# Sparse attention's second half in a given order on TensorE, with fixed score banks, and an earlier end of the state-space preparation

## The chip, the cores and the metric

The kernel runs on one NeuronCore of a Trainium2 chip. A core has TensorE for matrix products and transposes (PE; its weight loads stand in the profile as PEld), VectorE (DVE), ScalarE (ACT), GpSimd (POOL), the queue engine SyncE (SP), which issues most of the DMAs, and 16 DMA engines. Each engine works through its own queue in order, and semaphores tie the queues together. The metric is the device time of one launch in microseconds (us), lower is better.

## The reference, cut to what matters

The program is one block with a dilated-window attention and a pooling branch, followed by two layers of a second block. For 512 tokens of width 1024, all in float32, the stages that matter here are these two of the second block.

```python
# layer 0: sparse attention, 16 heads of 64, rows in 4 blocks of 128 queries
s = einsum('bqhd,bqkhd->bqhk', q, k[idx]) * HEAD_DIM_2 ** -0.5   # idx: the chosen keys
s = where(valid, s, NEG); p = softmax(s)
o = einsum('bqhk,bqkhd->bqhd', p, v[idx]); x = x + g_m * (o @ attn_w_out)
x = x + g_f * conv_ffn(h, ...)           # up, 3-tap convolution, silu gate, down
# layer 1: state-space mixer, then conv_ffn again
decay = exp(a_re * dt); ab = decay * (cos + i sin)(a_im * dt); bb = coef * b
x_t = ab * x_{t-1} + bb @ u_t;  y_t = Re(c @ x_t) + d * u_t
x = x + g_m * glu(gelu(y));  x = x + g_f * conv_ffn(h, ...)
```

In the kernel the choice of keys is a bias per query block (0 for a chosen key, -1e30 for another) that is added to the scores of all keys up to the block's end.

## The kernel before, in words

Activations lie feature-major: X is 8 tiles of 128 features x 512 tokens. A large product takes both operands in two parts (high and low) and adds three products per pair, at lines 260 to 262 in `mm3`; `gemm` does 24 of these for one 128x1024 weight tile and 18 for a 128x768 one. `weight` (lines 239 to 247) loads a tile on the SP queue, ACT makes the high part `wh`, DVE the low part `wl`. There are 4 raw buffers and 3 pairs of weight buffers, so the loads run some tiles ahead.

**The order of work.** The source is traced in order, and a scheduler then places the instructions of each engine by its own model of times; `tc.issue_after` ties an instruction on one engine behind another one. On the chip each engine follows the order that came out. Work in the background is a generator: `pump` (line 223), called once per `weight`, advances it by `rate` steps, and `finish` runs off what is left.

**Sparse attention** (`dsa`). For a head pair `pr` (0 to 7) and a query block `n` (3 to 0, with W = 128(n+1) keys) a unit is: `scores` (line 899), two products of 64 rows into two PSUM banks (L905), on DVE bias and row maximum (L914), a small operation for the exponent's shift (L919), on ACT exp with its row sum (L920), on DVE a reciprocal (L921), on POOL the scaling (L922); then `values` (line 932), transposes (L939), a copy to SBUF by ACT for one head and DVE for the other (L942, L944), the value products (L950), and ACT and DVE make the high and low part of the result (L955, L956). `attend` (line 960) runs `scores` of a unit and `values` of the unit two before. Pairs 0 to 3 run between the projections of the second half of q, k and v (PSUM pool pb); pairs 4 to 7 follow (scores in pool pa), then the 8 output products with `awo` (line 990).

**Preparation for layer 1** (`ssm_prep`, line 1060) computes the discrete system, then for each of the 8 feature tiles k fills `res` and `taps` and writes them to a DRAM tile: 8 transposes (L1195), 8 products in 4 column strips (L1201), a 1.5 MB write (L1212) and 16 small ones (L1216). By the source it yields some 100 steps. It is background of layer 0's feed-forward `conv_ffn(0)`, whose two loops take 44 up and 24 down weight tiles:

```python
bg.append(ssm_prep(sp, dp, rho))
rate[0] = 1.0
nxt = SumSq()
conv_ffn(0, up, acc, nxt)
finish()
```

**State-space mixer** (`s5`, line 1219). The matrices come back as `Rf` and `Rb_` (R in the trace; k = 0 to 2 by the ACT queue, the others by SP, L1229, L1231). The norm of X is: squares on ACT (L282), column sums on PE (L314), small steps on DVE (L297 to L336), a broadcast on PE (L319), a copy `Rb` (L327). Then `ahead` scales and shifts a tile (L1257 or L1259, L1261), PE reorders it (L1245), ACT copies it to U (L1278), and PE multiplies U by the matrices (L1284), the first product of the mixer proper.

## Time and profile before

| | |
|---|---|
| three runs | 2416.22, 2419.20, 2420.52 us; median 2419.2 |
| profiled execution | 2419.24 us, its span 2417.3 us (1.9 us lie around it) |
| PE busy | 2316.2 us (96%), weight loads 1882.7 us (78%) |
| DVE, ACT, POOL busy | 1436.1 us (59%), 876.1 us (36%), 503.0 us (21%) |
| mean granted clock of TensorE | 0.978 |
| chain that ended last | PE 87%, DVE 6%, DMA 3% |

An engine's busy time is the union of its instructions' spans. A PE instruction's end is modelled, so that a PE that waits a little between short products can still show as busy; start times are the better guide there, and the idle time of the weight loads. A line such as L260 belongs to a helper and stands for many stages, so stages are told apart by stretches of time: the second half of the attention is 1362 to 1432 us, layer 0's feed-forward 1468 to 1846, the mixer's start 1846 to 1889, the mixer 1889 to 2041.

### The profile page before, as it was taken

The numbers are of one execution on the slowest core, as the hardware profiler recorded it, in microseconds if no ns is written. First come the engines' busy times: TensorE is split into PE (matmuls) and PEld (weight loads), VectorE is DVE, ScalarE is ACT, GpSimd is POOL, SyncE is SP. The second block draws the span as 40 slices with busy tenths as digits, with TensorE's granted clock in tenths as the row PEclk, the third lists the DMA queues.
The fourth block names the chain that finished last, engine by engine and source line by source line (L and its number), as shares of the span: only waits on it lengthen the run. The fifth ranks groups of instructions, "written<-read, shape, count | busy, mean of one in ns | idle before, by whom it ended". The sixth has DMA issues, their size and how long they took to land.

```text
span 2417.3 us, 30042 instructions
## 1 busy us (share of the span) xinstructions
PE 2316.2 (96%) x11288; PEld 1882.7 (78%) x11288; DVE 1436.1 (59%) x2575; ACT 876.1 (36%) x1374; POOL 503.0 (21%) x462
## 2 busy tenths in 40 slices
PE   7999999999999999998999998999997699999999
PEld 6888888977888888887676577888786687888887
DVE  6655555456675555446797649747476664544443
ACT  3322233533333223234334644425254432433332
POOL 2312022241112212033001221302022520111111
PEclk9999999999999999998999999999998899999999
DMA  5444445323444444322221112333335622232332
GB/s 190 157 157 148 148 136 171 115 90 107 152 153 139 149 156 148 122 88 72 79 62 44 36 46 86 96 126 127 121 112 184 243 66 88 87 96 96 96 96 79
DMA packets 95618, 281.88 MB, mean 117 GB/s; under 512 B 11377, under 2 KB 16369, under 8 KB 93425
## 3 DMA queue, kind: packets, MB, share of 16 engines
q1 hardware_dynamic: 92160, 272.48, 34.9%
q10 hardware_dynamic: 3312, 7.48, 0.9%
q8 instruction: 89, 1.46, 0.2%
q14 instruction: 57, 0.46, 0.1%
HBM read 263.14 MB, written 16.78 MB: 116 GB/s over the span
## 4 chain that ended last, share of the span: by engine, by line
PE 87%; DVE 6%; DMA 3%; issue 1%; ACT 1%; POOL 1%; SPq 1%; ACTq 0%; DVEq 0%; POOLq 0%
PE pa L260 27%; PE pa L261 27%; PE pa L262 27%; DMA raw<-in_ada 1%; PE pb L950 1%; PE pb L939 1%; PE pa L905 1%; DMA dr<-sm 1%; DVE wl L246 1%; PE pb L905 1%; SPq L1216 1%; ACT wh L245 0%; PE pb L314 0%; PE pa L557 0%; PE pb L1284 0%
## 5 line engine op out<-in xcount | busy, mean ns | idle before, releaser
L245 ACT ACTIVATE wh<-raw 128x1024 fp32r<-128x1024 f32 (+2 forms) x380 | 392.1, 1035 | 856.4 <-PE pa L261 680.5
L260 PE MATMUL pa<-x,wh 128*128 128x512 f32 x1736 | 679.5, 393 | 14.4 <-ACT x L343 8.1
L261 PE MATMUL pa<-x,wh 128*128 128x512 f32 x1736 | 680.4, 392 | 4.5 <-DVE x L344 4.5
L262 PE MATMUL pa<-x,wl 128*128 128x512 f32 x1736 | 677.7, 391 | 0.5 <-DVE wl L246 0.5
L246 DVE TENSOR_TENSOR wl<-raw,wh 128x1024 fp32r<-128x1024 f32 (+2 forms) x380 | 494.1, 1302 | 244.8 <-ACT wh L245 236.1
L260 PEld LDWEIGHTS pa<-x,wh 128*128 128x128 f32 x1736 | 327.7, 189 | 85.9 <-ACT x L343 8.1
L261 PEld LDWEIGHTS pa<-x,wh 128*128 128x128 f32 x1736 | 327.6, 189 | 75.6 <-DVE x L344 7.7
L262 PEld LDWEIGHTS pa<-x,wl 128*128 128x128 f32 x1736 | 327.7, 189 | 68.8 <-DVE wl L246 1.0
L261 PE MATMUL pa<-u,wh 128*128 128x512 f32 x704 | 274.7, 391 | 0.0
L260 PE MATMUL pa<-u,wh 128*128 128x512 f32 x704 | 273.7, 392 | 0.0
L262 PE MATMUL pa<-u,wl 128*128 128x512 f32 x704 | 273.1, 391 | 0.0
L368 DVE SCALAR_TENSOR_TENSOR ada<-raw,c,ada 128x512 f32<-128x512 f32 x168 | 130.7, 778 | 220.2 <-DMA raw<-in_ada 219.3
L1013 POOL TENSOR_TENSOR t<-t,t 128x512 f32<-128x512 f32 x44 | 70.8, 1610 | 534.7 <-ACT t L1012 534.7
L402 POOL TENSOR_TENSOR t<-t,t 128x512 f32<-128x512 f32 x44 | 70.5, 1601 | 497.7 <-DVE t L401 272.3
L260 PE MATMUL pa<-wh,x 128*128 128x512 f32 (+1 forms) x384 | 151.0, 401 | 14.6 <-DVE t L805 6.1
L260 PEld LDWEIGHTS pa<-u,wh 128*128 128x128 f32 x704 | 132.2, 188 | 29.8 <-ACT wh L245 1.3
L262 PEld LDWEIGHTS pa<-u,wl 128*128 128x128 f32 x704 | 132.2, 188 | 28.9 <-issue 0.4
L261 PEld LDWEIGHTS pa<-u,wh 128*128 128x128 f32 x704 | 132.3, 188 | 28.3 <-POOL u L406 0.2
L262 PE MATMUL pa<-wh,x 128*128 128x512 f32 (+1 forms) x384 | 150.5, 394 | 0.0
L261 PE MATMUL pa<-wl,x 128*128 128x512 f32 (+1 forms) x384 | 149.7, 390 | 0.0
L1023 DVE SCALAR_TENSOR_TENSOR x<-pa,c,x 128x512 f32<-128x512 f32 x48 | 35.4, 748 | 137.7 <-PE pa L262 137.7
L288 POOL TENSOR_TENSOR acc<-acc,t 128x512 f32<-128x512 f32 x45 | 75.4, 1681 | 179.8 <-ACT t L282 169.4
(365 smaller groups left out, 2739.9 us busy)
## 6 DMA issues: line engine op xcount, KB each, us to landing
raw<-in_ada SPq DMA_DIRECT2D x96, 512.0 KB, 3.8
raw<-in_u SPq DMA_DIRECT2D x88, 512.0 KB, 3.5
raw<-in_f1u SPq DMA_DIRECT2D x44, 512.0 KB, 3.8
raw<-in_f2u SPq DMA_DIRECT2D x44, 512.0 KB, 3.6
raw<-in_d SPq DMA_DIRECT2D x32, 512.0 KB, 3.5
raw<-in_aq SPq DMA_DIRECT2D x28, 512.0 KB, 3.8
dr<-res SPq DMA_DIRECT2D x8, 1536.0 KB, 7.1
raw<-in_wpg SPq DMA_DIRECT2D x20, 512.0 KB, 3.6
```

What stands on the lines that cost most here:

```text
L245: S.activation(h[:, :w], r[:, :w], AF.Copy)
L246: eng.tensor_tensor(l[:, :w], r[:, :w], h[:, :w].bitcast(F32), op=ALU.subtract)
L260: E.matmul(ps, ah, bh, start=first, stop=False)
L261: E.matmul(ps, ah, bl, start=False, stop=False)
L262: E.matmul(ps, al, bh, start=False, stop=last)
L288: G.tensor_tensor(self.sums[0], self.sums[0], sq, op=ALU.add)
L368: V.scalar_tensor_tensor(acc, r[:, j * T : (j + 1) * T], kk, acc, op0=ALU.mult, op1=ALU.add)
L402: G.tensor_tensor(b, a, b, op=ALU.mult)
L905: E.matmul(ps[e][:, :W], QT[pr][base : base + 64, n * P : (n + 1) * P], KTT[pr][base : base + 64, :W], start=True, stop=True,)
L939: E.transpose(p[:, j * P : (j + 1) * P], s[:, j * P : (j + 1) * P], ident)
L1013: G.tensor_tensor(b, a, b, op=ALU.mult)
L1023: V.scalar_tensor_tensor(X[m], p, MOD[i][:, 40 + m : 41 + m], X[m], op0=ALU.mult, op1=ALU.add)
```

## The change

In the second half of the attention (pairs 4 to 7) three things change. Score banks are two fixed pairs, taken once from pool pa and used in turn (`pairs`). `values` is split into `turn` (transposes and copies) and `mix` (value products), and PE gets a written order by `tc.issue_after`: scores of unit u, transposes of unit u-3, value products of unit u-4. The exponents of these pairs go to tiles of pool `du` instead of the ring `s` of 5. In both halves the two heads of a unit share the small tile `mx`: one DVE operation of 128x2 for both shifts and one for both reciprocals, after both maxima and both exponents; the maximum of head 1 is taken before that of head 0. Apart from that the background rate of `ssm_prep` goes from 1.0 to 1.7 steps per weight tile.

```diff
@@ scores
-                    ps = [psb() if pr < 4 else psa() for _ in range(2)]
+                    if pr < 4:
+                        ps = [psb() for _ in range(2)]
+                    else:
+                        ps = pairs[(4 * pr + n) % 2]
...
+                    ss = [ds_.tile([P, T], F32, name=nm("s"), tag="s", bufs=5) if pr < 4 else ut() for _ in range(2)]
+                    mx = ds_.tile([P, 4, 2], F32, name=nm("mx"), tag="mx", bufs=4)
+                    for e in (1, 0):
+                        V.tensor_tensor_reduce(
+                            out=ss[e][:, :W], in0=ps[e][:, :W], in1=bias[n], scale=1.0, scalar=-3e38,
+                            op0=ALU.add, op1=ALU.max, accum_out=mx[:, 0, e : e + 1],
+                        )
+                    sc = rq[:, n, 2 * pr : 2 * pr + 2]
+                    V.scalar_tensor_tensor(mx[:, 1], mx[:, 0], -1.0, sc, op0=ALU.mult, op1=ALU.mult)
                     for e in range(2):
...
+                        S.activation(
+                            ss[e][:, :W], ss[e][:, :W], AF.Exp, bias=mx[:, 1, e : e + 1], scale=sc[:, e : e + 1],
+                            accum_out=mx[:, 2, e : e + 1],
                         )
...
+                    V.reciprocal(mx[:, 3], mx[:, 2])
+                    for e in range(2):
+                        G.tensor_scalar(ss[e][:, :W], ss[e][:, :W], mx[:, 3, e : e + 1], 1.0, op0=ALU.mult, op1=ALU.mult)
+                    return ss, last
@@ after the projections
-                for pr in range(4, 8):
-                    for n in (3, 2, 1, 0):
-                        attend(pr, n)
-                while pend:
-                    values(*pend.pop(0))
+                pairs += [[psa() for _ in range(2)] for _ in range(2)]
+                tail = [(pr, n) for pr in range(4, 8) for n in (3, 2, 1, 0)]
+                last, turned = None, []
...
+                while tail or pend or turned:
+                    if tail:
+                        with after():
+                            ss, last = scores(*tail[0])
+                        pend.append((*tail.pop(0), ss))
+                    if len(pend) > 3 or not tail:
...
+                        with after():
+                            pts, last = turn(*pend[0])
+                        turned.append((*pend.pop(0)[:2], pts))
+                    if len(turned) > 1:
+                        with after():
+                            last = mix(*turned.pop(0))
@@ the program's end
                 bg.append(ssm_prep(sp, dp, rho))
-                rate[0] = 1.0
+                rate[0] = 1.7
```

In the order of PE inside the attention's second half, before: score products are L905 (pa), transposes L939, value products L950.

```order
L905 MATMUL pa_10857<-du_9654,du_10169 128x256
L950 MATMUL pb_10819<-pt_10812,du_10479 64x128
L939 MATMUL pb_10844<-c_102,s_10756 128x128
L905 MATMUL pa_10858<-du_9654,du_10169 128x256
L950 MATMUL pb_10819<-pt_10817,du_10479 64x128
L950 MATMUL pb_10819<-pt_10812,du_10480 64x128
L950 MATMUL pb_10819<-pt_10817,du_10480 64x128
L939 MATMUL pb_10848<-c_102,s_10763 128x128
L905 MATMUL pa_10900<-du_9654,du_10169 128x128
L950 MATMUL pb_10852<-pt_10846,du_10479 64x128
L939 MATMUL pb_10875<-c_102,s_10795 128x128 x4
L905 MATMUL pa_10901<-du_9654,du_10169 128x128
```

Between the two score products of a unit (pa_10857 and pa_10858, pa_10900 and pa_10901) stand value products and transposes of other units.

And with the change (L909, L944 and L960 are the same three):

```order
L944 MATMUL pb_10756<-c_102,du_10645 128x128
L944 MATMUL pb_10758<-c_102,du_10646 128x128
L960 MATMUL pb_10764<-pt_10730,du_10431 64x128
L960 MATMUL pb_10764<-pt_10732,du_10431 64x128
L960 MATMUL pb_10764<-pt_10730,du_10432 64x128
L960 MATMUL pb_10764<-pt_10732,du_10432 64x128
L909 MATMUL pa_10447<-du_9642,du_10133 128x128
L909 MATMUL pa_10448<-du_9642,du_10133 128x128
L944 MATMUL pb_10784<-c_102,du_10677 128x128 x4
L944 MATMUL pb_10789<-c_102,du_10678 128x128 x4
L960 MATMUL pb_10798<-pt_10760,du_10431 64x128
L960 MATMUL pb_10798<-pt_10762,du_10431 64x128
```

The two score products of a unit (pa_10447 and pa_10448) now stand side by side, and so do its transposes and its value products.

PE at the end of layer 0's feed-forward, before. L262 is the last product of the feed-forward, L1195 and L1201 are the preparation of tiles 5 to 7, L314 and L319 the norm.

```order
L262 MATMUL pa_14521<-u_14256,wl_14518 128x512
L1195 MATMUL pb_14624<-c_102,pB_14605 128x128 x4
L1195 MATMUL pb_14630<-c_102,pB_14606 128x128 x4
L1201 MATMUL pb_14636<-mC_14607,pB_14605 32x128 x4
L1201 MATMUL pb_14636<-mC_14608,pB_14606 32x128 x4
L1195 MATMUL pb_14740<-c_102,pB_14721 128x128 x4
L1195 MATMUL pb_14746<-c_102,pB_14722 128x128 x4
L1201 MATMUL pb_14752<-mC_14723,pB_14721 32x128 x4
L1201 MATMUL pb_14752<-mC_14724,pB_14722 32x128 x4
L1195 MATMUL pb_14802<-c_102,pB_14783 128x128 x4
L1195 MATMUL pb_14808<-c_102,pB_14784 128x128 x4
L1201 MATMUL pb_14814<-mC_14785,pB_14783 32x128 x4
```

Of the eight rounds of preparation, the last three stand behind the feed-forward's last product; the third begins with the last three of these rows.

And with the change (the preparation's lines would be L1227 and L1233):

```order
L260 MATMUL pa_14699<-u_14488,wh_14695 128x512
L261 MATMUL pa_14699<-u_14489,wh_14695 128x512
L262 MATMUL pa_14699<-u_14488,wl_14696 128x512
L314 MATMUL pb_14770<-c_78,acc_14518 128x1 x4
L314 MATMUL pb_14770<-c_78,t_14691 128x1 x4
L314 MATMUL pb_14770<-c_78,t_14719 128x1 x4
L319 MATMUL pb_14799<-c_102,c_14787 128x128 x4
L1277 MATMUL pb_14828<-t_14822,c_102 32x128 x16
```

The three rounds are gone from there; the last round now stands 11 weight tiles before the feed-forward's end, and all eight lie inside.

ACT at the same place, before: L327 is the copy of the norm's broadcast, L1261 the scaled tiles, the DMAs are the loads of R for k = 0 to 2, L1278 the copy to U.

```order
L327 ACTIVATE rb_14928<-pb_14923 128x512
L1261 ACTIVATE t_14946<-t_14944,c_108,c_8103 128x512
L1261 ACTIVATE t_14950<-t_14948,c_108,c_8103 128x512
L1261 ACTIVATE t_14983<-t_14981,c_108,c_8103 128x512
L1261 ACTIVATE t_15037<-t_15035,c_108,c_8103 128x512
L1229 DMA R_14850<-dr_12986 128x2048
L1231 DMA R_14852<-dr_12986 128x1536
L1229 DMA R_14854<-dr_13276 128x2048
L1231 DMA R_14856<-dr_13276 128x1536
L1229 DMA R_14858<-dr_13876 128x2048
L1231 DMA R_14860<-dr_13876 128x1536
L1278 ACTIVATE U_14954<-pb_14952 128x512
```

The six loads stand behind the scaled tiles and in front of the first U.

And with the change (L245 is the high part of the third tile of `glu`, L282 the square of the last X tile, L1317 a copy of the decay rates):

```order
L245 ACTIVATE wh_15597<-raw_15595 128x1024
L1261 DMA R_14726<-dr_12398 128x2048
L1263 DMA R_14728<-dr_12398 128x1536
L282 ACTIVATE t_14719<-x_100 128x512
L1261 DMA R_14730<-dr_12556 128x2048
L1263 DMA R_14732<-dr_12556 128x1536
L1261 DMA R_14734<-dr_13000 128x2048
L1263 DMA R_14736<-dr_13000 128x1536
L1317 ACTIVATE rt_14762<-c_11281 128x4x127
L1317 ACTIVATE rt_14763<-c_11281 128x4x127
L327 ACTIVATE rb_14804<-pb_14799 128x512
L1293 ACTIVATE t_14822<-t_14820,c_108,c_8103 128x512
```

Now they stand behind a weight copy, in front of the norm's last square or right behind it.

## Rows read from the trace of the kernel before

**Rows 1.** stretches: us, PE, PEld, DVE, ACT, POOL busy (count), PEclk, DMA share, GB/s.
```profile
1362.00:1407.00 45.00, 43.34 (x281) 25.31 (x280) 28.64 (x147) 30.98 (x93) 15.41 (x29) 0.96 0.00 1
...
1470.00:1846.00 376.00, 375.06 (x1708) 304.18 (x1707) 254.11 (x519) 158.53 (x228) 82.37 (x49) 1.00 0.35 114
1846.00:1889.00 43.00, 16.06 (x132) 12.06 (x130) 20.12 (x67) 16.92 (x30) 3.94 (x9) 0.56 0.59 213
```

**Rows 2.** timeline at the seam: start us, us, engine, line, operation [idle before <-releaser].
```profile
1845.17 0.39 PE L262 MATMUL pa<-u,wl 128*128 128x512 f32 x1
...
1845.42 1.06 ACT L245 ACTIVATE wh<-raw 128x1024 fp32r<-128x1024 f32 x1 [0.41 <-PE pa L261]
...
1847.35 0.74 DVE L1023 SCALAR_TENSOR_TENSOR x<-pa,c,x 128x512 f32<-128x512 f32 x1
```

**Rows 3.** the same timeline, further on.
```profile
1871.19 2.05 PE L319 MATMUL pb<-c,c 128*128 128x128 f32 x8 [3.90 <-DVE c L306]
...
1873.97 0.69 DVE L1257 TENSOR_TENSOR t<-x,pb 128x512 f32<-128x512 f32 x1 [2.63 <-ACT rb L327]
1874.76 4.91 ACT L1261 ACTIVATE t<-t,c,c 128x512 f32<-128x512 f32 x4 [0.89 <-DVE t L1257]
...
1876.12 1.93 PE L1245 MATMUL pb<-t,c 128*32 128x128 f32 x32 [2.88 <-ACT t L1261]
...
1879.06 0.33 ACTq L1229 DMA_DIRECT2D R<-dr  x1
...
1888.64 0.60 ACT L1278 ACTIVATE U<-pb 128x512 f32<-128x512 f32 x1 [8.97 <-issue]
...
1889.29 3.78 PE L1284 MATMUL pb<-U,R 128*128 128x128 f32 x16 [11.24 <-ACT U L1278]
```

**Rows 4.** timeline of the norm before the feed-forward of layer 1.
```profile
2043.74 0.63 ACT L282 ACTIVATE t<-x 128x512 f32<-128x512 f32 x1 [1.15 <-DVE x L1371]
...
2044.42 1.05 PE L314 MATMUL pb<-c,t 128*128 128x1 f32 x8 [1.06 <-ACT t L282]
...
2047.89 2.07 PE L319 MATMUL pb<-c,c 128*128 128x128 f32 x8 [2.42 <-DVE c L306]
```

**Rows 5.** PE timeline around one round of preparation inside the feed-forward.
```profile
1786.31 0.39 PE L262 MATMUL pa<-x,wl 128*128 128x512 f32 x1
1786.55 1.03 PE L1195 MATMUL pb<-c,pB 128*128 128x128 f32 x8
...
1787.65 0.39 PE L261 MATMUL pa<-x,wh 128*128 128x512 f32 x1
...
1792.66 0.39 PE L262 MATMUL pa<-x,wl 128*128 128x512 f32 x1
1792.98 0.64 PE L1201 MATMUL pb<-mC,pB 128*32 128x128 f32 x16
...
1793.89 0.40 PE L261 MATMUL pa<-x,wh 128*128 128x512 f32 x1
```

**Rows 6.** PE timeline, a score pair of the first half.
```profile
1241.84 1.13 PE L905 MATMUL pb<-du,du 64*128 64x512 f32 x4
```

**Rows 7.** PE timeline, score products of the second half.
```profile
1390.70 0.70 PE L905 MATMUL pa<-du,du 64*128 64x256 f32 x2
...
1394.31 1.12 PE L905 MATMUL pa<-du,du 64*128 64x512 f32 x2
```

**Rows 8.** lines of 1362 to 1407 us: busy us, mean ns, idle before <-releasers.
```profile
L920 ACT ACTIVATE s<-s,mx,sm 128x512 f32<-128x512 f32 x8 | 6.5, 813 | 4.5 <-DVE mx L919 2.3 <-PE pb L939 1.7 <-DVE mx L921 0.5
...
L922 POOL TENSOR_SCALAR s<-s,mx 128x512 f32<-128x512 f32 x8 | 5.6, 697 | 9.7 <-DVE mx L921 5.1 <-DVE mx L919 4.6
L914 DVE CUSTOM_DVE_ANT_0 s<-pa,sm 128x512 f32<-128x512 f32 x8 | 5.5, 688 | 2.1 <-PE pa L905 1.3 <-PE pb L939 0.8
```

**Rows 9.** a line of DVE inside the feed-forward, 1470 to 1846 us.
```profile
L1037 DVE TENSOR_TENSOR st<-sm,ca 128x128 f32<-128x128 f32 x12 | 4.2, 354 | 0.0
```

**Rows 10.** the same line behind the feed-forward, 1846 to 1889 us.
```profile
L1037 DVE TENSOR_TENSOR st<-sm,ca 128x128 f32<-128x128 f32 x4 | 1.1, 277 | 0.0
```

More of the change, by code (lines that the diff above doesn't have):

```diff
@@ L897, in project @@
                             S.activation(dst[4 * o + i][:, b * P : (b + 1) * P], p[:, i * P : (i + 1) * P], AF.Copy)
+                pairs = []
                 def scores(pr, n):
                     W = (n + 1) * P
-                    units = []
-                    ps = [psb() if pr < 4 else psa() for _ in range(2)]
+                    if pr < 4:
+                        ps = [psb() for _ in range(2)]
+                    else:
+                        ps = pairs[(4 * pr + n) % 2]
                     for e in range(2):
                         base = 64 * e
-                        E.matmul(
+                        last = E.matmul(
                             ps[e][:, :W], QT[pr][base : base + 64, n * P : (n + 1) * P], KTT[pr][base : base + 64, :W],
@@ L930, in carry, with turn, mix @@
                     S.activation(X[k], X[k], AF.Copy, scale=col("fn", k))
-                def values(pr, n, units):
+                def turn(pr, n, units):
                     W = (n + 1) * P
-                    pts = []
+                    ps, pts = [], []
                     for e in range(2):
-                        s = units[e]
                         p = psb()
                         for j in range(n + 1):
-                            E.transpose(p[:, j * P : (j + 1) * P], s[:, j * P : (j + 1) * P], ident)
+                            last = E.transpose(p[:, j * P : (j + 1) * P], units[e][:, j * P : (j + 1) * P], ident)
+                        ps.append(p)
+                    for e in range(2):
                         pt = ds_.tile([P, T], F32, name=nm("pt"), tag="pt", bufs=4)
                         if e == 0:
-                            S.activation(pt[:, :W], p[:, :W], AF.Copy)
+                            S.activation(pt[:, :W], ps[e][:, :W], AF.Copy)
                         else:
-                            V.tensor_copy(pt[:, :W], p[:, :W])
+                            V.tensor_copy(pt[:, :W], ps[e][:, :W])
                         pts.append(pt)
+                    return pts, last
+                def mix(pr, n, pts):
                     po = psb()
@@ L949, in values @@
                             hd = 2 * pr + e
-                            E.matmul(
+                            last = E.matmul(
                                 po[64 * e : 64 * e + 64, :P], VV[hd // 8][j][:, hd % 8 * 64 : hd % 8 * 64 + 64],
@@ L956, in values @@
                     V.tensor_tensor(OL[pr][:, sl], po[:, :P], OH[pr][:, sl].bitcast(F32), op=ALU.subtract)
+                    return last
+                def values(pr, n, units):
+                    mix(pr, n, turn(pr, n, units)[0])
                 pend = []
                 def attend(pr, n):
-                    pend.append((pr, n, scores(pr, n)))
+                    pend.append((pr, n, scores(pr, n)[0]))
                     if len(pend) > 2:
@@ L984, in dsa, with after @@
                 OL += [xt(F32R) for _ in range(4)]
-                for pr in range(4, 8):
-                    for n in (3, 2, 1, 0):
-                        attend(pr, n)
-                while pend:
-                    values(*pend.pop(0))
+                pairs += [[psa() for _ in range(2)] for _ in range(2)]
+                tail = [(pr, n) for pr in range(4, 8) for n in (3, 2, 1, 0)]
+                last, turned = None, []
+                def after():
+                    return nullcontext() if last is None else tc.issue_after(last.ins)
+                while tail or pend or turned:
[4 more added lines that the diff above has]
+                    if len(pend) > 3 or not tail:
+                        if not pend:
+                            with after():
+                                last = mix(*turned.pop(0))
+                            continue
+                        with after():
+                            pts, last = turn(*pend[0])
+                        turned.append((*pend.pop(0)[:2], pts))
+                    if len(turned) > 1:
+                        with after():
+                            last = mix(*turned.pop(0))
                 for m in range(KT):
```

14 lines of the change are left out of this document (removed).

## The prediction

> **What bounds the kernel now.** The table says PE is busy for 96% of the span, so I first ask where it is not, and read the view by stretches of time. In the feed-forward of layer 0 PE is busy for 375 of 376 us and DVE for 254: PE is the limit there. In the attention's second half PE counts as busy for 43.3 of 45 us, ACT, next, for 31.0. Behind the feed-forward, 1846 to 1889 us, PE is busy for 16 of 43 us, at a granted clock of 0.56 (mostly the lower of its two levels, 1.2 GHz), and nothing else is near its limit [rows 1]. I call this stretch the seam. Such a stretch is bounded by a chain, so I read its timeline.
>
> The last feed-forward product ends at 1845.17 + 0.39 = 1845.56 [rows 2]; the mixer's first product L1284 starts at 1889.29 [rows 3]: 43.7 us. What stands between is mostly the preparation, three of whose eight rounds of PE work are queued behind the feed-forward. DVE adds the last piece of X only at 1847.35 [rows 2], PE broadcasts the norm (L319) only at 1871.19, and ACT, ready for U since its scaling, first issues loads of R, from 1879.06 on, and gets to U at 1888.64 after 8.97 us of "issue" [rows 3]. By the order, the third of these loads waits for the last transfers of the preparation.
>
> **Part 1: the rate 1.7.** The feed-forward takes 44 + 24 = 68 weight tiles and the preparation some 100 steps; at 1.0 it cannot end in time, at 1.7 it has 116. The order shows the result: all rounds inside, the last 11 tiles before the end. Three effects.
>
> (a) The seam shrinks to the norm's own chain. Its new start: the weight copy L245 starts at 1845.42 and takes 1.06, so ACT is free at 1846.48; the addition to X, no longer behind preparation on DVE, takes 0.74 from 1845.56 and is done by 1846.30 [rows 2]. ACT issues two loads of R, 0.33 and about 0.4 us [rows 3], so the square starts near 1847.2. For the norm I take the same chain where it runs undisturbed, ahead of layer 1's feed-forward: square at 2043.74, column sums at 2044.42, broadcast at 2047.89, so 4.15 us [rows 4]. That puts the broadcast at 1851.35. From there on I keep the distances of the seam: broadcast 1871.19, scaling L1261 at 1874.76, L1245 at 1876.12, so 4.93 us; L1245 takes 1.93; and from U to L1284 it is 0.65 [rows 3]. In all 1851.35 + 4.93 + 1.93 + 0.65 = 1858.9. The seam falls from 43.7 to 13.3 us: **-30.4**. The four other loads of R stand between the square and the copy of the broadcast on ACT; at 0.33 to 0.7 each [rows 3] they are over before the broadcast lands 2.07 us [rows 4] after its start. The products behind the seam I leave at their present pace.
>
> (b) Three more rounds run inside the feed-forward, where PE is full, and there each product costs its time. At 376 us for 1708 groups [rows 1] two products start 0.22 us apart. Around the transposes L1195, L262 at 1786.31 to L261 at 1787.65 is 1.34, with two such steps 0.44 of it; around L1201 1792.66 to 1793.89 is 1.23, again less 0.44 [rows 5]. So 0.90 + 0.79 = 1.7 a round: **+5.1** for three.
>
> (c) DVE's preparation moves in too. All DVE work of the seam is 20.1 us, some 17 of it preparation by my estimate, and brings 254 to 271 of 376 us [rows 1]. That leaves it a quarter idle; weights are loaded tiles ahead, so the delays stay under cover. I take **0**; if the cover fails where steps bunch, all of the 17 us bounds it. SP is passed by the R loads of k = 0 to 2 only, and the three 1.5 MB writes join an average of 114 GB/s [rows 1]: nothing.
>
> One point speaks against moving DVE work next to GpSimd's. The same addition L1037 takes 354 ns inside the feed-forward [rows 9], where GpSimd is busy for 82 us, and 277 behind it [rows 10]. At 77 ns for each of the seam's 67 instructions [rows 1] DVE gets 5.2 us longer, still hidden. The Trainium skill, page "SBUF — State Buffer", section "SBUF: two separate sides", states that a DVE instruction with two SBUF inputs and a GpSimd one that reads SBUF share a port pair as an exclusive lock, and that the loser blocks for the other's whole instruction. The rows agree in sign; if every instruction met that block, DVE would lose what rival B works out.
>
> **Part 2: the attention.** (d) Score pairs. Two products of 64 rows that stand side by side run together: such a pair of 512 columns took 1.13 us [rows 6], a lone product 1.12 [rows 7]. By the order, 7 of the 16 pairs of the second half stood apart: three of 512 columns, two of 256, two of 128. The second of each costs about its own time: 3 x 1.12 + 4 x at most 0.70 [rows 7] = 6.2 at most, since the narrowest take less. This is the gain of the fixed pairs. (e) The written order puts three units' work between scores and transposes. The 16 units take the 45 us of the stretch [rows 1], 2.8 a unit, 8.4 for three. The chain of a unit at its widest: scores 1.1; two maxima of 0.69; two exponents of 0.81, two scalings of 0.70 [rows 8], about 0.5 for small steps: 6.0. It fits, with 2.4 to spare, though maxima and exponents of both heads now go ahead of the reciprocal. (f) Sharing takes away half of the 64 small DVE operations here, and DVE is busy for 28.6 of 45 us [rows 1]: nothing by itself. The first half of the attention sees only this sharing, with PE filled by projections: 0, by 3 either way.
>
> Bounds of the part: ACT's 31.0 us [rows 1] is a floor near 31, so at best -13.4; if ACT or DVE come late now and then, I give +3. I take **-6**, near the pairs' own price (d), because it is the one gain that rows show.
>
> **The sum.** -30.4 + 5.1 - 6 = -31.3 against the profiled execution's 2419.2, which is also the median: 2387.9, say **2388**. Only 0.2% (4.8 us) is about what a measurement tells from no change.
>
> **Rivals.**
> A. The loads of R become the wait. By the order they are 3 x 128 x 3584 floats, 5.5 MB, and now go out together near 1847. At the seam's mean of 213 GB/s [rows 1] they take 25.8 us; if they share the rate evenly the mixer starts near 1872.9 and not 1858.9: 2402. Against it: the first load was issued at 1879.06 and used at 1889.29 [rows 3], 10.2 us, and the new chain leaves 11.7. Chance 0.10.
> B. DVE falls behind inside the feed-forward. If every instruction moved met GpSimd as it is busy there, 82.4 of 376 us in 49 instructions of 1.7 us [rows 1], and waited half of one, that is 67 x 0.22 x 0.84 = 12 us of DVE; with 17 of its own bunched over weights that PE is waiting for, some 10 reach PE: 2398. Against it: the 105 us that DVE has left. Chance 0.08.
> C. Slower: the written order makes PE wait. PE can no longer slip other work in; if a unit's chain is longer than three units' work, the chain sets the pace, a third of it per unit. The gains without the attention are 25.3, so the total turns slower where 16 units take over 45 + 25.3 = 70.3 us, 4.4 a unit: a chain of 13.2 us. At 14.5 it gives 16 x 4.83 = 77.3, +32.3 for the attention: 2419.2 - 25.3 + 32.3 = 2426. Against it: 6.0 by the rows; for it: ACT and DVE also copy and split in between, and serve in order. Chance 0.04.
> D. The attention gets down to ACT's floor: -13 and not -6, so 2381. For it: less work in small pieces on PE; against it: ACT would have to run without a gap. Chance 0.07.
> That the rate does nothing is excluded by the order, which has no preparation behind the feed-forward.
>
> **How the numbers follow.** The forecast has 0.71, A 0.10, B 0.08, C 0.04, D 0.07. The forecast's own range is 2380 to 2397: 3 us below for the first half or the seam and 5 for an attention at -11, the other way 9 for an attention at +3. With A and D and a little around them the range is **2378 to 2403**; C and the outer tails are left out. Faster by over 0.2%: all but C, 0.96, less 0.03 for A and B together with a poor attention, which end within 0.2%: 0.93, 0.03 and, for C, 0.04.
>
> **What would show it.** Right: no L1195 or L1201 of the preparation (under its new numbers) behind the feed-forward; a seam of 12 to 15 us; the feed-forward some 5 us longer; the attention's second half near 38 us, its score pairs all of one product's time. A shows as the first mixer product waiting for a load of R, B as feed-forward products waiting for DVE's `wl`, C as transposes L944 waiting for GpSimd's scaling in each unit. The forecast is wrong if the seam stays above 20 us, or if the second half of the attention takes more than 48.

## The result, and the profile after

The changed kernel takes 2388.3 us in the median where the kernel before takes 2419.9: a ratio of 0.987, 95% interval 0.985 to 0.989, so it is faster by 1.3%. Its undisturbed runs are 2384.5, 2388.3 and 2390.3 us (one more ran at a granted clock of 0.56 throughout and is left out). The prediction was 2388, range 2378 to 2403.

I cut both profiled executions at the same products and compare the stretches. The loads ahead of the first products take 39 or 44 us from run to run whatever the kernel, so the first cut is the 29th product of L260.

| stretch, us | before | after | difference |
|---|---|---|---|
| start to the 29th product of L260 | 39.6 | 43.9 | +4.3, by chance |
| from there to layer 0's feed-forward (the attention lies at its end) | 1429.0 | 1418.4 | -10.6 |
| feed-forward, first to last product | 376.5 | 382.6 | +6.1 |
| seam, last product's start to the mixer's first | 44.1 | 13.4 | -30.7 |
| from there to the end | 528.0 | 530.1 | +2.1 |

The second of these stretches holds far more than the attention, so I cut it further, at three products that both kernels have. Between them PE does the same number of products in both kernels. The first is the first score product of the attention's first half, the second the last projection product ahead of pair 4, the third the last output product:

```profile
1241.84 1.13 PE L905 MATMUL pb<-du,du 64*128 64x512 f32 x4
...
1353.46 0.40 PE L262 MATMUL pa<-wh,x 128*128 128x512 f32 x1
...
1457.60 0.40 PE L262 MATMUL pa<-x,wl 128*128 128x512 f32 x1
```

and in the changed kernel:

```profile
1244.32 1.13 PE L909 MATMUL pb<-du,du 64*128 64x512 f32 x4
...
1354.21 0.40 PE L262 MATMUL pa<-wh,x 128*128 128x512 f32 x1
...
1451.42 0.40 PE L262 MATMUL pa<-x,wl 128*128 128x512 f32 x1
```

The first half goes from 111.6 to 109.9 us (-1.7), the second half with the output products from 104.1 to 97.2 (-6.9): -8.6 in all. The other 2 of the -10.6 lie mostly ahead of the attention, where single traces differ by as much whatever the kernel.

The view by stretches of the changed kernel, with the columns of [rows 1]: the attention's second half from its first score product to the output products, the feed-forward, the seam.

```profile
1362.00:1401.00 39.00, 36.28 (x278) 21.85 (x279) 27.14 (x127) 29.79 (x95) 15.41 (x31) 0.96 0.01 1
1470.00:1845.00 375.00, 373.95 (x1755) 302.17 (x1754) 257.27 (x551) 164.87 (x245) 77.41 (x55) 1.00 0.38 130
1845.00:1858.20 13.20, 6.85 (x66) 5.90 (x64) 4.62 (x15) 7.65 (x10) 3.75 (x3) 0.69 1.01 415
```

In the seam the DMA engines are now full, at 415 GB/s, where the long seam before had 213 [rows 1]. Its timeline, which answers to [rows 2, 3]:

```profile
1844.86 0.39 PE L262 MATMUL pa<-u,wl 128*128 128x512 f32 x1
...
1845.10 1.06 ACT L245 ACTIVATE wh<-raw 128x1024 fp32r<-128x1024 f32 x1 [2.56 <-PE pa L261]
1845.12 0.33 ACTq L1261 DMA_DIRECT2D R<-dr  x1
1845.29 0.75 DVE L1055 SCALAR_TENSOR_TENSOR x<-pa,c,x 128x512 f32<-128x512 f32 x1 [2.08 <-PE pa L262]
...
1846.13 0.63 ACT L282 ACTIVATE t<-x 128x512 f32<-128x512 f32 x1
...
1850.38 2.05 PE L319 MATMUL pb<-c,c 128*128 128x128 f32 x8 [2.51 <-DVE c L306]
...
1855.30 1.94 PE L1277 MATMUL pb<-t,c 128*32 128x128 f32 x32 [2.87 <-ACT t L1293]
1857.55 0.61 ACT L1310 ACTIVATE U<-pb 128x512 f32<-128x512 f32 x1
...
1858.21 2.08 PE L1316 MATMUL pb<-U,R 128*128 128x128 f32 x8 [0.98 <-ACT U L1310]
```

The last product of the feed-forward ends at 1845.25. ACT splits the weight (L245), issues loads of R at once, squares the last X at 1846.13, the broadcast is at 1850.38, L1277 (L1245 before) at 1855.30 and the first product at 1858.21, 13.0 us behind the last one's end. That is the chain of the prediction, step by step, and the first product waits for U, not for R. Two small misses offset each other: the square starts 0.88 us behind the last product's end where 1.64 were forecast, since the first loads are issued while the weight copy still runs, and from L1277 to the first product it takes 2.91 where 2.58 were forecast.

The attention's second half, PE's timeline. A score or value product shows as x2 here. The rows are the first unit's wait and the score pair behind it, value products of a narrow unit (two of them, x4) with the next score pair, and value products of a wide unit (eight, x16) with what follows them.

```profile
1368.56 0.49 PE L909 MATMUL pa<-du,du 64*128 64x128 f32 x4
1370.77 1.33 PE L944 MATMUL pb<-c,du 128*128 128x128 f32 x8 [1.72 <-POOL du L929]
...
1372.56 2.08 PE L909 MATMUL pa<-du,du 64*128 64x512 f32 x4
...
1382.56 0.44 PE L960 MATMUL pb<-pt,du 128*64 128x128 f32 x4
1382.93 1.13 PE L909 MATMUL pa<-du,du 64*128 64x512 f32 x4
...
1384.85 1.09 PE L960 MATMUL pb<-pt,du 128*64 128x128 f32 x16
1385.87 0.92 PE L909 MATMUL pa<-du,du 64*128 64x384 f32 x4
```

And the kernel before: four score products of three units in one group (512, 384, 384 and 256 columns), the wait of another, and one unit's value products (L950) in two pieces.

```profile
1364.22 1.77 PE L905 MATMUL pa<-du,du 64*128 64x512 f32 x8
...
1368.84 0.49 PE L905 MATMUL pa<-du,du 64*128 64x128 f32 x2 [1.27 <-DVE mx L914]
...
1384.52 0.43 PE L950 MATMUL pb<-pt,du 128*64 128x128 f32 x2
1384.88 0.87 PE L939 MATMUL pb<-c,s 128*128 128x128 f32 x6
1385.69 1.09 PE L950 MATMUL pb<-pt,du 128*64 128x128 f32 x14
1386.71 0.92 PE L905 MATMUL pa<-du,du 64*128 64x384 f32 x4
```

Before, one value product went ahead alone and kept PE for 0.36 us (1384.52 to 1384.88); the other seven took 1.02. In the changed kernel all eight of such a unit take 1.02 (1384.85 to 1385.87). So the eighth costs nothing in company: the two heads' value products of 64 columns run side by side, two taking 0.37 us (1382.56 to 1382.93) where one alone takes 0.36.

### The profile page after: what moved, and what is told of

Its sections match the earlier page's. It is cut to its first block, busy times and chain, and to the rows that moved or that the text cites. A ratio compares the mean times of both kernels' runs of the same rounds, so it can differ in the third digit from the quotient of the medians.

```text
span 2388.3 us, 29925 instructions
## 1 busy us (share of the span) xinstructions
PE 2316.5 (97%) x11288; PEld 1882.9 (79%) x11288; DVE 1425.1 (60%) x2511; ACT 873.6 (37%) x1374; POOL 501.1 (21%) x462
## 4 chain that ended last, share of the span: by engine, by line
PE 91%; DVE 5%; ACT 2%; issue 1%; DMA 1%; POOL 1%; SPq 0%; ACTq 0%; DVEq 0%; POOLq 0%
PE pa L260 28%; PE pa L261 27%; PE pa L262 27%; PE pb L960 1%; PE pb L314 1%; PE pa L1374 1%; PE pb L1316 1%; PE pb L944 1%; DMA raw<-in_ada 1%; PE pb L909 1%; PE pb L319 0%; PE pa L557 0%; PE pa L909 0%; DVE x L723 0%; PE pb L841 0%
## 5 line engine op out<-in xcount | busy, mean ns | idle before, releaser
L245 ACT ACTIVATE wh<-raw 128x1024 fp32r<-128x1024 f32 (+2 forms) x380 | 392.0, 1035 | 880.4 <-PE pa L261 685.5
L260 PE MATMUL pa<-x,wh 128*128 128x512 f32 x1736 | 682.4, 395 | 12.5 <-ACT x L343 8.1
L262 PE MATMUL pa<-x,wl 128*128 128x512 f32 x1736 | 679.6, 392 | 0.5 <-DVE wl L246 0.5
L260 PEld LDWEIGHTS pa<-x,wh 128*128 128x128 f32 x1736 | 329.1, 190 | 84.5 <-ACT x L343 8.1
L262 PEld LDWEIGHTS pa<-x,wl 128*128 128x128 f32 x1736 | 328.9, 189 | 69.2 <-DVE wl L246 1.0
L260 PE MATMUL pa<-u,wh 128*128 128x512 f32 x704 | 274.7, 393 | 0.0
L262 PE MATMUL pa<-u,wl 128*128 128x512 f32 x704 | 273.4, 391 | 0.0
L260 PE MATMUL pa<-wh,x 128*128 128x512 f32 (+1 forms) x384 | 152.1, 404 | 13.1 <-DVE t L805 6.6
L260 PEld LDWEIGHTS pa<-u,wh 128*128 128x128 f32 x704 | 132.1, 188 | 30.9 <-ACT wh L245 2.2
L262 PEld LDWEIGHTS pa<-u,wl 128*128 128x128 f32 x704 | 132.3, 188 | 28.8 <-issue 0.2
L262 PE MATMUL pa<-wh,x 128*128 128x512 f32 (+1 forms) x384 | 150.9, 395 | 0.0
L260 PEld LDWEIGHTS pa<-wh,x 128*128 128x128 f32 x384 | 85.3, 223 | 31.0 <-issue 10.6
```

The source lines that it names most:

```text
L245: S.activation(h[:, :w], r[:, :w], AF.Copy)
L260: E.matmul(ps, ah, bh, start=first, stop=False)
L262: E.matmul(ps, al, bh, start=False, stop=last)
```

## The experiments

From each run's trace I took the same stretches, and within the attention's second half the time from each product's start to the next one's, added up over the score products (S), transposes (T) and value products (M) from pair 4 to the feed-forward. A product's share so holds the wait of the product behind it, too. At the rate 1.7 the feed-forward repeats within 2 us from trace to trace; the long stretch to the feed-forward differs by 2.6 between the kernel before and e1, which are the same up to there. So a second table has the attention's two halves alone, cut as above; there the runs with the same order agree within 0.3 us. All ratios are to the kernel before, with 95% intervals; those of neighbours overlap often, and then the stretches decide.

| run | median us | ratio | to the feed-forward | feed-forward | seam | S, T, M |
|---|---|---|---|---|---|---|
| kernel before | 2419.9 | 1 | 1429.0 | 376.5 | 44.1 | 19.4, 12.8, 16.6 |
| the change | 2388.3 | 0.985 to 0.989 | 1418.4 | 382.6 | 13.4 | 16.0, 13.9, 13.1 |
| e1 rate only | 2396.6 | 0.989 to 0.992 | 1426.3 | 381.6 | 13.3 | 19.3, 13.0, 16.6 |
| e2 attention only | 2413.4 | 0.996 to 0.998 | 1417.5 | 377.7 | 43.8 | |
| e3 no written order | 2387.1 | 0.985 to 0.988 | 1418.0 | 382.2 | 13.4 | 15.7, 12.0, 13.2 |
| e4 pairs broken | 2394.3 | 0.990 to 0.996 | 1451.2 | 382.3 | 13.3 | |
| e5 ring of 5 | 2388.2 | 0.986 to 0.989 | 1422.4 | 381.6 | 13.4 | 19.9, 12.2, 13.4 |
| e6 tiles only | 2394.5 | 0.987 to 0.991 | 1424.3 | 381.5 | 13.7 | 15.7, 11.9, 17.7 |
| e7 two units behind | 2389.0 | 0.986 to 0.989 | 1417.4 | 382.3 | 13.3 | 17.9, 12.5, 13.1 |
| e8 rate 4.0 | 2396.6 | 0.989 to 0.992 | 1418.6 | 392.2 | 13.8 | |
| e9 no fixed banks | 2385.2 | 0.984 to 0.987 | 1418.0 | 382.4 | 13.3 | 16.2, 11.5, 13.2 |
| e10 no sharing | 2390.2 | 0.986 to 0.989 | 1418.3 | 383.5 | 13.8 | 15.4, 11.3, 13.2 |
| e11 R loads reversed | 2393.4 | 0.988 to 0.991 | 1418.4 | 382.6 | 18.5 | |
| e12 rate 1.2 | 2406.8 | 0.993 to 0.996 | 1418.0 | 387.8 | 28.0 | |

| run | first half, us | second half with output products, us | granted clock in the second half |
|---|---|---|---|
| kernel before, e1 | 111.6, 111.6 | 104.1, 104.1 | 0.984, 0.984 |
| the change, e2, e8, e11, e12 | 109.9 to 110.0 | 97.1 to 97.4 | 0.982 |
| e3 no written order | 109.9 | 95.5 | 1.000 |
| e4 pairs broken | 109.9 | 130.4 | 0.764 |
| e5 ring of 5 | 109.9 | 99.7 | 1.000 |
| e6 tiles only | 111.6 | 101.2 | 1.000 |
| e7 two units behind | 109.9 | 97.8 | 1.000 |
| e9 no fixed banks | 109.9 | 95.6 | 1.000 |
| e10 no sharing | 111.6 | 95.7 | 1.000 |

The clock is part of these differences. In the kernel before and in the change it falls to its lower level for 3 to 4 us behind a wait of PE (1.27 and 1.72 us, the rows above), and in the change the score pair behind it takes 2.08 us instead of 1.13. By the mean clock this costs 0.016 x 104 = 1.7 us before and 0.018 x 97 = 1.7 in the change, an estimate.

### The two halves of the change apart

**e1**, on the kernel before:

```diff
-                rate[0] = 1.0
+                rate[0] = 1.7
```

> The kernel before with the rate 1.7 and nothing else. If the parts add up as in the prediction: the seam goes from 43.7 to 13 us (-30) and the feed-forward of layer 0 gets 5 us longer, the attention stays: 2419 - 25 = about 2394 us. Rival (the attention's new order makes the room for the preparation): the seam shrinks less than 25 us, over 2400. Rival (the attention's change brings nothing that lasts to the end): about 2389, as fast as the whole change.

Measured 2396.6, 23.3 us less, 1.7 short of the 25 expected. The seam falls to 13.3 us without the attention's part. Its timeline, with the lines of the kernel before:

```profile
1851.16 0.40 PE L262 MATMUL pa<-u,wl 128*128 128x512 f32 x1
...
1856.69 2.05 PE L319 MATMUL pb<-c,c 128*128 128x128 f32 x8 [2.52 <-DVE c L306]
...
1864.50 1.86 PE L1284 MATMUL pb<-U,R 128*128 128x128 f32 x7 [0.96 <-ACT U L1278]
```

**e2**, on the changed kernel:

```diff
-                rate[0] = 1.7
+                rate[0] = 1.0
```

> The changed kernel with the rate back at 1.0, so the attention's changes alone. If the parts add up: the second half of the attention 6 us and the output products 2 us shorter, the seam at 43 us: about 2411 to 2413 us. Rival (the attention only shifts its waits to the norm or the feed-forward behind it): 2417 to 2421, no change that can be measured.

Measured 2413.4, 6.5 us less than before, and the seam is back at 43.8 us. The two parts give 23.3 + 6.5 = 29.8, the whole 31.6: they add up within the runs' scatter. The rate is about three quarters of it.

### What of the attention's part works

**e3**, on the changed kernel:

```diff
                 def after():
-                    return nullcontext() if last is None else tc.issue_after(last.ins)
+                    return nullcontext()
```

> The changed kernel without issue_after, all else kept (fixed banks, shared small operations, the same source order): the scheduler again puts other work between the two score products of 6 of 16 units (one of 512, two of 256, three of 128 columns) where the changed kernel has 2 (512 and 256). Theory, broken pairs cost a product each: about 0.6 + 3 x 0.4 = 2 us more, 2391. Rival, the order itself (three units between scores and transposes) is the gain: the attention's gain of 6 to 8 us is gone, about 2396.

Both were wrong, as 2387.1 is no slower than the change, and the second half is even 1.7 us shorter, 95.5 against 97.2. That is not because broken pairs are free; two things offset each other. The order makes PE wait 1.72 us for the first unit's scaling, and behind that wait the change runs at the lower clock for a while (the estimate of 1.7 us above), where e3 stays at 1.00. Against that, e3's score products cost some 0.9 us more by themselves (worked out under (d)).

**e4**: `scores` takes a step `mid` as an argument, the `turn` of the unit three before, and does it, in the written order, behind its first product:

```diff
                     for e in range(2):
                         base = 64 * e
-                        last = E.matmul(
...
+                        with after() if mid else nullcontext():
+                            last = E.matmul(
...
+                        if mid:
+                            LAST[0] = last
+                            if e == 0:
+                                mid()
```

> The changed kernel with a written order that puts the transposes of unit u-3 between the two score products of unit u, so that all 16 pairs stand apart and nothing else is different. Theory, a pair side by side takes the time of one product: the 14 pairs newly broken cost 3 x 1.05 + 4 x 0.85 + 3 x 0.62 + 4 x 0.41 = 10 us, 2399 us, all of it between the first score product and the output products. Rival, PE waits for the chain of exponents and the pairs are hidden by that: under 3 us, 2389 to 2392.

The times fall in two groups: seven of 2388 to 2394 us (median 2392.6) and five of 2416 to 2421. The profile is of the second group. By stretches (columns as before):

```profile
1362.00:1372.00 10.00, 9.08 (x55) 4.97 (x54) 5.85 (x31) 8.03 (x25) 3.22 (x6) 0.97 0.00 1
1372.00:1382.00 10.00, 10.00 (x33) 4.93 (x32) 3.09 (x11) 3.80 (x11) 1.65 (x4) 0.50 0.01 2
...
1422.00:1432.00 10.00, 10.00 (x40) 5.69 (x39) 3.55 (x16) 4.49 (x14) 2.50 (x4) 0.50 0.00 0
1432.00:1470.00 38.00, 37.55 (x195) 28.57 (x194) 14.29 (x26) 11.97 (x24) 7.25 (x8) 0.99 0.17 56
```

TensorE was granted the lower level, 0.50, for 61 us from about 1371.3 on, until the output products ran. The mean clock of the whole run is 0.970 to 0.972 in the five and 0.984 in all of the seven, so the 27 us between the two groups' medians go with the clock. The other group, where the pairs' price would stand alone, is 4.3 us above the change: neither the 10 expected nor the rival's under 3. By themselves this order's score products take some 9 us more than the change's (worked out under (d)), and some of it may be offset by what the change pays for its first wait and its clock. I have no trace of that group, so this was not seen.

**e5**, on the run without the written order:

```diff
-                    ss = [ds_.tile([P, T], F32, name=nm("s"), tag="s", bufs=5) if pr < 4 else ut() for _ in range(2)]
+                    ss = [ds_.tile([P, T], F32, name=nm("s"), tag="s", bufs=5) for _ in range(2)]
...
-                    if len(pend) > 3 or not tail:
+                    if len(pend) > 2 or not tail:
```

> The run without the written order again, but with the exponents of pairs 4 to 7 back in the ring of 5 tiles (two and a half units), and the transposes two units behind in the source; fixed banks and shared operations stay. Theory, the ring held PE back: a unit keeps its two tiles for some 7 us, so 2.5 units in 7 us are 2.8 us a unit, the pace of the kernel before; the attention's gain goes again: +6 to +8 on 2387, 2393 to 2395. Rival, broken pairs: 7 pairs stand apart (four of 512, three of 256) where that run has 6 narrower ones, +2.6: 2390. Rival, the fixed banks or the shared operations made the gain: 2387.

The second half gets 4.2 us longer, 99.7 against 95.5, and the score products' share goes from 15.7 back to 19.9 us: about half of the attention's gain goes, not all of it. But two things changed at once, as the transposes are also one unit nearer to the scores. The transposes of the widest unit now wait for GpSimd's scaling three times, 1.9 us in all, and the score products stand further apart (some 2.7 us). What the ring alone costs was not separated. The median moved by 1.1 only, within the scatter.

**e6**, on e1:

```diff
-                        s = ds_.tile([P, T], F32, name=nm("s"), tag="s", bufs=5)
+                        s = ds_.tile([P, T], F32, name=nm("s"), tag="s", bufs=5) if pr < 4 else ut()
```

> The kernel before with the rate 1.7, and the exponents of pairs 4 to 7 in tiles of pool du and not in the ring of 5; no fixed banks, no shared operations, no written order. Theory, the ring held PE back: nearly all of the attention's gain, 2396.6 - 6 to 8 = 2389 to 2391. Rival, pairs side by side are the gain: 6 pairs stand apart where 7 did, at most 1 us: 2396. Rival, the shared operations or the fixed banks: 2396.

Score products fall from 19.3 to 15.7 us, and the second half from 104.1 to 101.2; of these 2.9 us some 1.7 are the clock, which stays at 1.00 here. The score products come in 13 groups instead of 19, and the waits in their share stay what they were (some 2.7 us). More than half of the gain stays out: value products are at 17.7 us, where every kernel that has `mix` apart from `turn` has 13.1 to 13.4.

**e9** and **e10**, both on the run without the written order. The first takes the fixed banks away, the second gives each head its own small operations again:

```diff
-                        ps = pairs[(4 * pr + n) % 2]
+                        ps = [psa() for _ in range(2)]
```

```diff
-                    mx = ds_.tile([P, 4, 2], F32, name=nm("mx"), tag="mx", bufs=4)
...
+                    for e in range(2):
+                        mx = ds_.tile([P, 4], F32, name=nm("mx"), tag="mx", bufs=8)
...
```

> The run without the written order, and without the fixed banks too: each unit of pairs 4 to 7 takes the next two banks of pool pa. Tiles of pool du and shared operations stay. From the first score product of pair 4 to the first product of the feed-forward that run took 98.2 us and the one with the tiles alone 102.8. If the fixed banks make this difference: 102 to 103 us there, 2391 to 2392 in all. If the shared operations do: 98 to 99 us, 2387.

> The run without the written order, and with each head's own small operations again in both halves (maximum, shift, exponent, reciprocal, scaling head by head). Tiles of pool du and fixed banks stay. If the shared operations make the difference between 98.2 and 102.8 us: 102 to 103 us from the first score product to the feed-forward, 2391 to 2392. If the fixed banks do: 98 to 99 us, 2387. By the prediction sharing is worth nothing, since DVE is busy for under two thirds of the stretch.

Neither is the cause: 97.7 and 97.1 us from the first score product of pair 4 to the feed-forward, where that run had 98.2. So in the second half fixed banks and shared operations each bring nothing by themselves. In the first half sharing does bring something: 109.9 to 110.0 us in every run that has it, 111.6 in all that do not, e10 among them, and PE's idle time there is 4.3 us instead of 7.5. What e3, e9 and e10 have and e6 lacks is the split of `values`, with the value products a step behind the transposes; e5 and e7, two units behind as e6, have it too, at 13.4 and 13.1. The split was not run by itself.

**e7**, on the changed kernel:

```diff
-                    if len(pend) > 3 or not tail:
+                    if len(pend) > 2 or not tail:
```

> The changed kernel with the transposes two units behind the scores in the written order, not three. By the prediction's chain of 6.0 us at the widest (4.7 in the mean) two units' work covers it nearly: 0 to 1 us, 2389 to 2390. By the changed kernel's own trace the first unit takes 8.2 us from its scores to its transposes: then PE waits some 2 to 3 us in each of the four groups of four units: +8 to +12, about 2399. With the clock as in the run with broken pairs, more.

The time does not move, 2389.0, but two units' work does not quite cover a chain. Ahead of the widest unit's transposes PE waits for GpSimd's scaling in each of the four groups of four units, 1.89 us in the first and 0.95 or 0.96 in the others:

```profile
1368.09 1.13 PE L909 MATMUL pa<-du,du 64*128 64x512 f32 x4
...
1373.99 1.32 PE L944 MATMUL pb<-c,du 128*128 128x128 f32 x8 [0.95 <-POOL du L929]
```

From this unit's scores to its transposes it is 5.9 us, the prediction's 6.0; the 8.2 us that I read from the first unit of the changed kernel belong to the pipeline's start. The second half takes 97.8 us at a clock of 1.00, the change's 97.2 with some 1.7 of it owed to the lower clock: so the third unit is worth some 2 us (an estimate), which the change gives back through its clock.

### The preparation's place

**e8**: `rate[0] = 4.0` in place of 1.7.

> The changed kernel with the rate 4.0: all of the preparation lies in the first 28 of 68 weight tiles. DVE has some 105 us of preparation (254 + 17 less 1.07 x 156 as in the feed-forward of layer 1) and 70 of its own in the 157 us that these tiles take. If DVE's cover holds only where it has idle time, as rival B has it, the feed-forward gets (175 - 157) = some 18 us longer: 2407. If the tiles loaded and split ahead cover it: 2389. The seam stays at 13 us either way.

The feed-forward takes 392.2 us, 9.6 more than at 1.7: about half of the bound. The waits of PE in it (engine, tile, line, what it waited for, us in total, times, longest):

```profile
PE pa L260 <- ACT u L1048: 3.7, 1, 3.7
PE pb L1233 <- ACT mC L1213: 2.9, 2, 2.7
```

PE waits for the gate (L1048) and for the preparation's own pieces, not for `wl`. At 1.7 the same view had no wait of this kind.

**e12**: `rate[0] = 1.2`.

> The changed kernel with the rate 1.2: by the order one round of preparation of eight is left behind the feed-forward, where the kernel before has three. By the prediction's terms a round costs 30.4 / 3 = 10 us behind the feed-forward and 1.7 inside: seam 23 us, feed-forward 1.7 us shorter, 2389 + 8.4 = 2398. Rival, the seam's price is a step (the end of the preparation's transfers, whatever their number): 30 us for the first round already, near 2415.

2406.8, between the two. PE also waited 4.3 us for the gate in the feed-forward, and the seam is 28.0 us with one round in it. Its timeline:

```profile
1854.25 13.57 SPq L1248 DMA_DIRECT2D dr<-sm  x16
...
1865.45 0.33 ACTq L1261 DMA_DIRECT2D R<-dr  x1
...
1872.88 0.33 ACTq L1261 DMA_DIRECT2D R<-dr  x1
...
1875.13 1.29 ACT L1293 ACTIVATE t<-t,c,c 128x512 f32<-128x512 f32 x1 [13.71 <-issue]
...
1876.96 1.44 PE L1316 MATMUL pb<-U,R 128*128 128x128 f32 x5 [13.54 <-ACT U L1310]
```

The 16 small writes of the one round leave SP over 13.6 us, up to 1867.8; ACT issues the second pair of R loads, which by the order waits for the preparation's last transfers, at 1872.88, and U stands behind it (13.71 us of "issue" ahead of L1293). So the first round left behind costs 28.0 - 13.4 = 14.6 us, and the next two, with the 44.1 of the kernel before, 8.0 each.

### The loads of R

**e11**: the tiles are taken for k = 0, 1, 2 as before, and the loads issued for k = 2, 1, 0:

```diff
-                for k in range(KT):
+                for k in (2, 1, 0, *range(3, KT)):
...
-                    q.dma_start(Rf, spill[k][:, :4])
...
-                    q.dma_start(Rb_, spill[k][:, 4:])
+                    q.dma_start(RR[k][0], spill[k][:, :4])
+                    q.dma_start(RR[k][1], spill[k][:, 4:])
```

> The changed kernel with the loads of R on ACT issued for k = 2, 1, 0 and not 0, 1, 2. In the changed kernel's trace they land 9.0, 12.8 and 16.4 us after their issues. If the transfers are served in the order of issue: the matrices of k = 0 land near 1863 and not 1854, the first mixer product waits for them and not for U, some 5 us later: seam 18 to 19 us, 2392 to 2395. If they share the rate evenly, as rival A had it, all land together and nothing changes: 13 us, 2389.

Served in order: 2393.4, and the first product waits for the load, 5 us longer.

```profile
1854.99 1.93 PE L1283 MATMUL pb<-t,c 128*32 128x128 f32 x32 [2.87 <-ACT t L1299]
1863.01 3.75 PE L1322 MATMUL pb<-U,R 128*128 128x128 f32 x16 [6.09 <-DMA R<-dr]
```

In the changed kernel itself the first load of k = 0, issued at 1845.12, landed 9.0 us later, 4.1 us ahead of its use; the first of k = 2 took 16.4. The rows are of the view of DMA issues, KB each, us to landing:

```profile
R<-dr ACTq DMA_DIRECT2D x1, 1024.0 KB, 9.0
...
R<-dr ACTq DMA_DIRECT2D x1, 1024.0 KB, 16.4
```

## Why the prediction was right

**(a) The seam: right.** -30.4 forecast, -30.7 measured, by the same steps. The norm ran in 4.25 us from square to broadcast (4.15 forecast), and 4.92 from there to L1277 (4.93).

**(b) Three rounds in the feed-forward: right in size.** +5.1 forecast; +6.1 by the whole change, +5.1 by the rate alone (e1), and 382.6 - 377.7 = +4.9 between the change and e2.

**(c) DVE under cover: right at 1.7, and e8 shows the end of it.** At 4.0 half of the bound appears, through ACT's and the preparation's own waits. DVE's busy time in the feed-forward rose only from 254.1 [rows 1] to 257.3 us and not to 271, so the cover was tested less than I thought. The price of 77 ns by which I judged the contention with GpSimd was off: the same addition inside the changed feed-forward (L1037 is L1069 there) takes what it took behind it before, 281 against 354 [rows 9] and 277 ns [rows 10].

```profile
L1069 DVE TENSOR_TENSOR st<-sm,ca 128x128 f32<-128x128 f32 x16 | 4.5, 281 | 0.0
```

So the stretch does not set it; what does was not found. The exclusive lock of the Trainium skill, page "SBUF — State Buffer", section "SBUF: two separate sides", may lie behind the 354; no run here isolated it.

**(d) The score pairs: the mechanism is real, but its size was wrong, and the forecast of -6 came close by luck.** The second half measured -6.9, and -6.5 is the attention's part in the median (e2). Products of 64 rows do run side by side, but this is worth some 2.5 us here and not 6. Group by group, from a group's start to the next product, score products without a wait and at the full clock take 0.21 us and 0.21 more per 128 columns in the busier half of the rows: 0.42, 0.63, 0.84 and 1.05 for 128 to 512 columns, alone or in a pair (a pair of 512 measured 1.06). This fits those groups of all traces within some 0.1 us. Added up by it, the score products alone take 15.7 us before, 13.2 in the change, 14.1 in e3, 16.8 in e5, 13.0 in e6 and 22.1 in e4, an estimate; what the S of the table has above that are waits and the lower clock.

The step that failed: I let the second product of each separated pair cost its full time. In the kernel before it often ran beside a product of another unit; the group of 1364.22 took 1.70 us to the next product, where 512, two of 384 side by side and 256 columns in turn would take 1.05 + 0.84 + 0.63 = 2.5. And the change leaves two pairs apart. The larger gain was not in the prediction: value products, 3.5 us of M (16.6 to 13.1). They run two by two as well, and a lone one has lost its partner: 0.36 us alone, nothing in company. They stand together since they come a step behind the copies they read (e3, e5, e7, e9, e10 against e6; the split not run alone). I put the gain on the fixed pairs of banks; e9 is as fast without them and without the written order. What brings score products closer is the tiles of `du` (e6: 13 groups for 19).

Each change from one kind of product to another costs something, too. The Trainium skill, page "TensorEngine Tiling (Array Packing)", section "Key Properties", says that a change of the tiling mode drains TensorE, and the three kinds of products here have three shapes (64 rows; all of the array; 64 columns). From pair 4 on they stand in 71 groups of one kind before, 72 in e6, 55 to 60 in the runs with the split. That agrees in direction; no run here isolated the switch.

**(e) The chain of 6.0 us: right** for the wide units, 5.9 in e7. That three units' work covers it holds but for the first unit, where PE waits 1.72 us; two units' work falls short by 0.95 a group of four. **(f) Sharing: right at zero in the second half, wrong in the first**, where it brings 1.7 us (e10), within the 3 that I allowed.

**The sum** of the profiled executions is +4.3 - 10.6 + 6.1 - 30.7 + 2.1 = -28.8; their times say -28.9 (2390.3 against 2419.2). The attention brought 8.6 us where 6 were forecast, and the feed-forward gives 1.0 back. The rest is scatter of single traces: ahead of the attention the stretch from the 29th product takes 1199 to 1203 us whatever the kernel, and the one behind the seam 527.7 to 530.4 (e12 and e7, with the same code there). That the median meets the forecast within 1 us is so in part luck, as these misses and the mis-sized (d) offset one another.

**The rivals.** A fell by its own premise: the loads are served in the order of issue at 415 GB/s and not evenly at 213, and e11 shows that they would decide if k = 0 came last. B needs a rate well above 1.7 (e8). C did not appear at three units behind but for the first unit's 1.72 us; at two it begins (e7). D was partly there: the second half came to 38.1 us of 44.4, not to ACT's 31.

The fastest median was e9's, 2385.2 us (0.984 to 0.987): no written order, no fixed banks, tiles of `du`, shared operations, rate 1.7. Its interval overlaps that of the change, so it is as fast and simpler, not shown faster.

## What to carry to other kernels

When background work is paced, add up what is left of it where its cover ends: a round here cost 1.7 us inside a full feed-forward and 8 to 15 behind it. Products that fill half of the array, by rows or by columns, are worth keeping next to another that fills the other half, whichever unit it belongs to. When they stand apart, ask first which buffer or copy made the scheduler put something between; moving the consumer one step later and giving the ring more tiles did as much here without a written order (e9). And where several loads are issued together, issue the one needed first, first.

## What the runs showed of the hardware

The granted clock can stay low for much longer than the gap that came ahead of it. In the change's own profile and in e4's, PE waited ahead of the first unit's transposes, 1.72 us and 0.91 us. The rows of e4, and the clock of the change by stretch:

```profile
1369.41 1.32 PE L953 MATMUL pb<-c,du 128*128 128x128 f32 x8 [0.91 <-POOL du L938]
...
1371.46 2.07 PE L914 MATMUL pa<-du,du 64*128 64x512 f32 x2
```

```profile
1372.00:1382.00 10.00, 9.64 (x73) 5.71 (x73) 5.96 (x24) 5.90 (x19) 3.50 (x7) 0.83 0.01 2
1382.00:1392.00 10.00, 9.50 (x84) 5.97 (x84) 8.08 (x40) 8.45 (x31) 4.45 (x9) 1.00 0.00 0
```

In the change the clock was 0.83 in the one stretch and 1.00 in the next; in five of twelve runs of e4 the time is 27 us longer, and the profiled one of these had 0.50 up to 1432.8 with PE counted as busy all the while. The score product at 1371.46 took 2.07 us where one takes 1.12 [rows 7]. And in e7, where PE waited 1.89 us at the same place, the clock stayed at 1.00:

```profile
1364.21 1.32 PE L944 MATMUL pb<-c,du 128*128 128x128 f32 x8 [1.89 <-POOL du L929]
```

```profile
1366.00:1376.00 10.00, 9.03 (x80) 5.53 (x80) 7.67 (x32) 7.29 (x24) 3.84 (x8) 1.00 0.01 2
```

What made the difference between the three was not settled.
